# Feed-forward matmuls of a two-layer transformer block in other orders: two passes swapped, two tiles side by side

## The chip, the cores and the metric

The kernel runs on one core of a Trainium2 chip. Its engines are TensorE (PE, with its weight loads as PEld), VectorE (DVE), ScalarE (ACT), GpSimd (POOL) and SyncE (SP, which here only starts transfers). Each takes its own instructions in order and waits for the others by semaphores. The metric is the device time of one execution, in microseconds.

## What is computed

A sequence of 512 tokens with 1024 features passes through two layers, each with attention and a feed-forward part, and a last norm. The change touches the feed-forward part alone:

```python
def conv_ffn(h, w_in, conv_w, conv_b, w_out):      # w_in 1024 x 5632, w_out 2816 x 1024
    u = h @ w_in
    up = jnp.pad(u, ((0, 0), (CONV_WIDTH - 1, 0), (0, 0)))
    c = conv_b + conv_w[0] * up[:, 0:s]
    for i in range(1, CONV_WIDTH):
        c = c + conv_w[i] * up[:, i:i + s]
    a, gate_in = jnp.split(c, 2, axis=-1)
    return (jax.nn.silu(a) * gate_in) @ w_out

h = h + conv_ffn(rms_norm(h, norm_ffn[layer]), ...)
```

## The kernel before

All activations lie with features on the 128 partitions and the 512 tokens along the free axis. Every operand of the large products is split in two parts, high and low, of a narrower kind of float (fp32r), and `mm3` (line 101) computes a product in three matmuls, or passes, that add up in one bank of PSUM: high by high (line 102), high weight by low activation (line 103), low weight by high activation (line 104). The weight is the stationary operand, so each pass loads it anew.

`weight` (line 110) brings one tile of 128 x 1024 weights: a transfer into `wr` (three buffers, line 115), a cast on ACT into the high part `wh` (three buffers, line 116), and a subtraction for the low part `wl` (three buffers, line 117), in the feed-forward of layer 1 always on POOL. A cast can start when the transfer has landed and PE has read the last of what the buffer held before.

`ffn` (line 378) runs for each layer. Its hidden features are done in two halves. In each half 11 pairs of tiles (a feature tile and its gate tile, `fin`) are multiplied with the normed input `x`, one weight tile after the other, 8 contraction chunks by 3 passes, so 24 matmuls of 512 columns to a weight tile; the pair's results lie in the two banks of one `pss` tile, which has two buffers. DVE scales them (line 412), ACT and DVE apply the convolution (lines 414 to 417), ACT the silu (line 420), and the product is split again into `actv` (lines 198 and 199). Then come the output products of that half (`product`, line 427): for each of 8 output tiles 11 chunks by 3 passes into one `pst` bank (three buffers), which DVE adds to `h` (line 443). Their weights (`fout`) are 11 tiles of 8 blocks each, block number f * 11 + k, so a weight tile serves parts of two output tiles.

The program is written in this order, and a scheduler then places the instructions of each engine: it may move some ahead of others when it expects an operand to be late. The result is a fixed order for each engine.

Of the kernel before, what the change touches and what calls it, by code (L numbers as in the profile page):

```python
# [17 lines left out]
P = 128  # L18
S = 512
D = 1024  # L20
NCH = D // P
# [12 lines left out]
# which of Pool (P) and DVE (V) takes a subtraction or sum that either can: the low parts of the weights, in  # L34
# order (layer 0, layer 1), and of other operands
# [4 lines left out]
# where the steps of the attention phases go among one another, in units of quads (four heads of a token tile)  # L40
# [10 lines left out]
# where the norm of the first half of the tokens goes in the products of the second half  # L51
# [4 lines left out]
# columns of the constant table  # L56
# [5 lines left out]
# columns of the mask table  # L62
# [10 lines left out]
def hybrid_kernel(ctx, tc, t):  # L73
# [73 lines left out]
    def warm_exp(dep):  # L147
        # the exponential's table, loaded ahead of its first use
        act(small.tile([P, 1], F32, name="warm", bufs=1), dep, AF.Exp, scale=0.0)

# [12 lines left out]
    def token_scale(ssq=None):  # L163
        """1 / rms of each token, [P, NT] with tokens on partitions."""
# [10 lines left out]
    def spread_scale(r_nat):  # L175
        """The same along the free axis, on every partition, in PSUM."""
        ps = t_tile()
        for i in range(NT):
            mm(ps[:, i * P:(i + 1) * P], r_nat[:, i:i + 1].to_broadcast([P, P]), ident, start=True, stop=True)
        return ps  # L180
# [7 lines left out]
    def weave(*lists):  # L188
        """Emit lists of steps side by side, each in its own order; (steps, first, last) places one."""
# [28 lines left out]
    # in four steps, one token tile and one bank each  # L218
# [22 lines left out]
    # or in four steps along the contraction, two token tiles to a bank  # L241
# [24 lines left out]
    def split_v(dst, src, r):  # L266
        # dst [P, g, 2, 64] f32r, src [P, g, 64] in PSUM
# [4 lines left out]
    def cat_k(pool, k, n):  # L272
        # k [P, n, 64] natural -> the same as hi|lo
# [4 lines left out]
    def stack_k(dst, kc, n):  # L278
        # -> dst [(hi|lo, d), n, P]
# [26 lines left out]
    def probs_t(pool, blocks, way="V"):  # L306
        # four [P, P] blocks -> split [key, head, query]
# [15 lines left out]
    def heads_out(pool, ot, pv, quad, i):  # L323
        # pv [(hi|lo, d), 4 heads * P] -> ot [(head parity, d), chunk, hi/lo, token]
# [11 lines left out]
    def out_proj(h, ot, ws, half, last):  # L336
# [21 lines left out]
        def early():  # L358
            # the first half of the heads, for four feature tiles
# [18 lines left out]
    def ffn(layer, gi, h, slots, before, last, end=None):  # L378
        with tc.tile_pool(name=f"ffn{layer}", bufs=1) as fp:
# [9 lines left out]
            for half in range(2):  # L389
                acts = []  # L390
                for j in range(HPAIR):
                    jj = half * HPAIR + j
                    ps = s_tile()
                    for s in range(2):
                        hi, lo = weight(t["fin"][layer, 2 * jj + s])
                        hv = hi.rearrange("p (k n) -> p k n", k=NCH)
                        lv = lo.rearrange("p (k n) -> p k n", k=NCH)
                        for c in range(NCH):
                            mm3(ps[:, s], hv[:, c], lv[:, c], x[c][:, 0], x[c][:, 1],
                                c == 0, c == NCH - 1)  # L400
                    if jj == 0:
# [4 lines left out]
                    for s in range(2):  # L406
                        src = ps[:, s]
                        if jj == 0:
                            # the scale comes later than the first pair
# [17 lines left out]
                def product(ps, f, toks, ks):  # L427
                    for k in ks:
# [4 lines left out]
                        col = slice(b % 8 * P, (b % 8 + 1) * P)  # L433
                        mm3(ps, hi[:, col], lo[:, col], acts[k][:, 0, toks], acts[k][:, 1, toks],
                            k == 0, k == HPAIR - 1)

                for f in range(NCH):
                    if half == 1 and f == NCH - 1 and end:
# [8 lines left out]
    # ================= layer 0 attention =================  # L447
    x = x_pair(["s1", "s2"])

    with tc.tile_pool(name="att_a", bufs=1) as pa, tc.tile_pool(name="att_a2", bufs=1) as pp:  # L450
# [9 lines left out]
        # one key-value group: its four query heads, and its keys and values of both branches  # L460
# [105 lines left out]
        def compress(kv):  # L566
# [50 lines left out]
            def third():  # L617
# [3 lines left out]
                # [Vh | Vl] below the blocks of hi and of lo probabilities, zero for the other head  # L621
# [32 lines left out]
        def quad_a(g, i):  # L654
            nb = i + 1
            # the compressed keys in front of the others, where they fit in the same banks
# [111 lines left out]
            def ctrans():  # L768
                # rows (head parity, hi/lo, block)
# [46 lines left out]
        def ahead(n):  # L816
            # the softmax of quad n, the queries of quad n + 1, the copy of those of quad n + 2
# [27 lines left out]
    # ================= layer 0 feed forward =================  # L845
# [5 lines left out]
    def after_a(f):  # L851
        # the inputs of layer 1, feature tile by feature tile
# [11 lines left out]
    # ================= layer 1 attention =================  # L864
# [121 lines left out]
    # ================= layer 1 feed forward and the final norm =================  # L986
# [4 lines left out]
    def finale(product):  # L991
        # the last feature tile in two halves of the tokens, and the norm of each at once
# [15 lines left out]
        def sums(a):  # L1008
            # the squares of the other feature tiles
# [94 lines left out]
def _halves(w):  # L1104
    # [1024, 1024] -> (half, f pair) tiles of [P, 2 f, 4 k, P]
# [4 lines left out]
def _layout(a):  # L1110
# [21 lines left out]
    # (a_j, gate_j) feature tiles in turn  # L1132
# [26 lines left out]
```

## Time and profile before

| what | value |
|---|---|
| runs | 1299.46 and 1537.13 us, median 1418.3 us |
| the profiled execution, its span | 1298.1 us |
| PE busy | 1251.8 us (96%) |
| weight loads on PE | 1041.9 us (80%) |
| DVE busy | 831.9 us (64%) |
| ACT busy | 629.9 us (49%) |
| POOL busy | 661.4 us (51%) |

Times in the trace count from the span's start. Layer 0's feed-forward takes about 375 to 740, layer 1's about 898 to 1290. A row of the timeline is an instruction (or several alike in a row) with its start, its duration and, in brackets, how long its engine had been idle and what ended that. Matmuls overlap, so the time that one takes of PE is the step from its start to the next one's. PEclk is the granted clock as a share of 2.4 GHz; 0.50 is 1.2 GHz.

### The profile page before, as it was taken

To read this page: it belongs to the slowest core of one execution; us is meant where nothing else is said; L and a number is where in the kernel's file an instruction comes from. 1 tells how busy PE (TensorE), PEld (TensorE's weight loads), DVE (VectorE), ACT (ScalarE), POOL (GpSimd) and SP (SyncE) were. 2 spreads that over 40 slices of the span, in tenths; PEclk is the share of its full clock that TensorE was granted. 3 is DMA by queue.
4 is the path that set the end of the run, shared out by engine and by line. 5 is a ranking of instruction groups with operands and counts; after the bars stand their busy time and mean duration, and the time that the engine had idled before them with its cause. 6 is when DMAs were issued, how large, how long until landed. Compare 5 with 4: busy or idle time off the path is not lost.

```text
span 1298.1 us, 17657 instructions
## 1 busy us (share of the span) xinstructions
PE 1251.8 (96%) x6539; PEld 1041.9 (80%) x6539; DVE 831.9 (64%) x1331; ACT 629.9 (49%) x1278; POOL 661.4 (51%) x536
## 2 busy tenths in 40 slices
PE   8988999999999999999999999899999999999997
PEld 7887787878778888888888898777788888888886
DVE  5877868787458775047776458775497730577712
ACT  4555867777454443124444347665454421344332
POOL 6425767766484444444445446664644444444452
PEclk9998999999999999999999999999999999999999
DMA  5342011121122222222222131111222222232221
GB/s 187 115 155 80 1 34 34 34 98 34 33 97 91 88 97 98 97 88 91 98 98 97 49 115 33 34 65 49 98 82 98 98 97 95 84 97 98 97 82 65
DMA packets 34085, 106.45 MB, mean 82 GB/s; under 512 B 4048, under 2 KB 6608, under 8 KB 34000
## 3 DMA queue, kind: packets, MB, share of 16 engines
q1 hardware_dynamic: 34000, 105.34, 24.1%
q8 instruction: 51, 0.84, 0.3%
q14 instruction: 34, 0.28, 0.1%
HBM read 103.23 MB, written 2.10 MB: 81 GB/s over the span
## 4 chain that ended last, share of the span: by engine, by line
PE 86%; DVE 8%; ACT 3%; issue 1%; DMA 1%; SPq 0%; POOL 0%; DVEq 0%; ACTq 0%; POOLq 0%
PE pss L103 14%; PE pss L104 14%; PE pss L102 14%; PE pst L102 10%; PE pst L104 10%; PE pst L103 10%; PE pst L310 3%; DVE s L185 2%; PE psv L765 1%; PE pss L713 1%; PE psv L764 1%; PE pss L714 1%; PE pst L300 1%; DVE s L347 1%; DVE nmx L725 1%
## 5 line engine op out<-in xcount | busy, mean ns | idle before, releaser
L117 POOL TENSOR_TENSOR wl<-wr,wh 128x1024 fp32r<-128x1024 f32 (+1 forms) x173 | 406.3, 2350 | 437.8 <-ACT wh L116 434.5
L116 ACT CAST wh<-wr 128x1024 fp32r<-128x1024 f32 (+2 forms) x201 | 197.7, 985 | 347.6 <-issue 173.1
L103 PE MATMUL pss<-s,wh 128*128 128x512 f32 x736 | 292.0, 397 | 3.8 <-DVE s L185 3.8
L102 PE MATMUL pss<-s,wh 128*128 128x512 f32 x736 | 291.3, 396 | 2.3 <-ACT s L198 2.1
L104 PE MATMUL pss<-s,wl 128*128 128x512 f32 x736 | 290.8, 396 | 0.0
L103 PEld LDWEIGHTS pss<-s,wh 128*128 128x128 f32 x736 | 138.3, 188 | 39.5 <-DVE s L185 6.2
L102 PEld LDWEIGHTS pss<-s,wh 128*128 128x128 f32 x736 | 138.1, 188 | 37.1 <-ACT s L198 3.0
L104 PEld LDWEIGHTS pss<-s,wl 128*128 128x128 f32 x736 | 138.3, 188 | 32.6
L104 PE MATMUL pst<-actv,wl 128*128 128x512 f32 (+1 forms) x363 | 141.0, 389 | 0.0
L103 PE MATMUL pst<-actv,wh 128*128 128x512 f32 (+1 forms) x363 | 140.7, 388 | 0.0
L102 PE MATMUL pst<-actv,wh 128*128 128x512 f32 (+1 forms) x363 | 140.3, 386 | 0.0
L415 DVE SCALAR_TENSOR_TENSOR cv<-u,convp,cv 128x512 f32<-128x512 f32 x88 | 123.2, 1439 | 13.4 <-ACT cv L414 13.4
L199 DVE TENSOR_TENSOR actv<-sa,actv 128x512 fp32r<-128x512 f32 x44 | 101.6, 2312 | 30.7 <-ACT actv L198 30.5
L443 DVE TENSOR_TENSOR s<-s,pst 128x512 f32<-128x512 f32 x31 | 21.3, 687 | 155.4 <-PE pst L104 155.4
L412 DVE TENSOR_TENSOR u<-pss,R 128x512 f32<-128x512 f32 x84 | 54.1, 686 | 64.5 <-PE pss L104 64.5
L420 ACT ACTIVATE sa<-cv 128x512 f32<-128x512 f32 x44 | 27.9, 634 | 123.1 <-DVE cv L417 123.0
L103 PEld LDWEIGHTS pst<-actv,wh 128*128 128x128 f32 x363 | 68.4, 188 | 15.2
L102 PEld LDWEIGHTS pst<-actv,wh 128*128 128x128 f32 x363 | 68.4, 188 | 14.8
L104 PEld LDWEIGHTS pst<-actv,wl 128*128 128x128 f32 x363 | 68.4, 188 | 13.9
L314 ACT CAST pth<-pst 128x512 fp32r<-128x512 f32 x92 | 53.7, 594 | 35.0 <-PE pst L310 30.9
L315 DVE TENSOR_TENSOR ptl<-pst,pth 128x512 fp32r<-128x512 f32 x92 | 62.2, 683 | 12.8 <-ACT pth L314 11.9
L414 ACT ACTIVATE cv<-u,convp 128x512 f32<-128x512 f32 x88 | 66.6, 807 | 2.2 <-DVE u L412 2.2
(242 smaller groups left out, 2634.4 us busy)
## 6 DMA issues: line engine op xcount, KB each, us to landing
wr<-fin SPq DMA_DIRECT2D x88, 512.0 KB, 3.3
wr<-fout SPq DMA_DIRECT2D x44, 512.0 KB, 3.2
wr<-wg SPq DMA_DIRECT2D x10, 512.0 KB, 3.3
wr<-cw SPq DMA_DIRECT2D x8, 512.0 KB, 3.4
wr<-woA SPq DMA_DIRECT2D x8, 512.0 KB, 3.8
wr<-woB SPq DMA_DIRECT2D x8, 512.0 KB, 3.3
wr<-wqb SPq DMA_DIRECT2D x6, 512.0 KB, 3.3
s<-xT SPq DMA_DIRECT2D x8, 256.0 KB, 5.3
```

The source lines that it names most:

```text
L102: mm(out, ah, bh, start=start, stop=False)
L103: mm(out, ah, bl, start=False, stop=False)
L104: mm(out, al, bh, start=False, stop=stop)
L116: nc.scalar.copy(hi[:, :n], raw[:, :n])
L117: engines[next(pick["w"], "P")].tensor_sub(lo[:, :n], raw[:, :n], hi[:, :n].bitcast(F32))
L199: engines[pick["split"][name] if name else "V"].tensor_sub(lo, src, hi.bitcast(F32))
L310: pe_tr(ps[:, r * P:(r + 1) * P], blocks[r], ident)
L314: nc.scalar.copy(ph, ps)
L315: nc.vector.tensor_sub(pl, ps, ph.bitcast(F32))
L412: nc.vector.tensor_mul(u[:, s, 2:], src, norm["R"])
L414: act(cv[:, s], u[:, s, 2:], AF.Identity, bias=par[:, 3:4], scale=par[:, 2:3])
L415: nc.vector.scalar_tensor_tensor(cv[:, s], u[:, s, 1:S + 1], par[:, 1:2], cv[:, s], op0=OP.mult, op1=OP.add)
```

## The change

Three places in `ffn` get another order; the arithmetic stays.

In layer 1 the first products of a pair are written side by side: for each chunk the passes are high by high, low weight by high, high weight by low, each for both tiles of the pair before the next pass, so that the two banks are written in turn. In layer 1's first half the output products are written in the same way for two output tiles at a time. In layer 0's first half the output products keep their one bank, but the second and third pass change places.

```diff
+                    pair = []
                     for s in range(2):
-                        hi, lo = weight(t["fin"][layer, 2 * jj + s])
-                        hv = hi.rearrange("p (k n) -> p k n", k=NCH)
-                        lv = lo.rearrange("p (k n) -> p k n", k=NCH)
+                        pair.append([z.rearrange("p (k n) -> p k n", k=NCH)
+                                     for z in weight(t["fin"][layer, 2 * jj + s])])
+                        if layer == 1:
+                            continue
+                        hv, lv = pair[s]
                         for c in range(NCH):
                             mm3(ps[:, s], hv[:, c], lv[:, c], x[c][:, 0], x[c][:, 1],
                                 c == 0, c == NCH - 1)
+                    if layer == 1:
+                        for c in range(NCH):
+                            for w, xx in ((0, 0), (1, 0), (0, 1)):
+                                for s in range(2):
+                                    mm(ps[:, s], pair[s][w][:, c], x[c][:, xx], start=c == 0 and (w, xx) == (0, 0),
+                                       stop=c == NCH - 1 and xx == 1)
...
+                        if half == 0 and layer == 0:
+                            mm(ps, hi[:, col], acts[k][:, 0, toks], start=k == 0, stop=False)
+                            mm(ps, lo[:, col], acts[k][:, 0, toks], start=False, stop=False)
+                            mm(ps, hi[:, col], acts[k][:, 1, toks], start=False, stop=k == HPAIR - 1)
+                            continue
                         mm3(ps, hi[:, col], lo[:, col], acts[k][:, 0, toks], acts[k][:, 1, toks],
                             k == 0, k == HPAIR - 1)

                 for f in range(NCH):
+                    if half == 0 and layer == 1:
+                        if f % 2:
+                            continue
+                        pq = [t_tile(), t_tile()]
+                        for k in range(HPAIR):
+                            for w, xx in ((0, 0), (1, 0), (0, 1)):
+                                for z in range(2):
+                                    b = (f + z) * HPAIR + k
+                                    if b // 8 not in wts:
+                                        wts[b // 8] = weight(t["fout"][layer, half, b // 8])
+                                    mm(pq[z], wts[b // 8][w][:, b % 8 * P:(b % 8 + 1) * P], acts[k][:, xx],
+                                       start=k == 0 and (w, xx) == (0, 0), stop=k == HPAIR - 1 and xx == 1)
+                        for z in range(2):
+                            nc.vector.tensor_add(h[:, f + z], h[:, f + z], pq[z])
+                        continue
```

How the instructions stand on PE and ACT shows what the scheduler made of it. In the rows below a name's number tells buffers' uses apart: a `wh` and the `wl` with the next number are the two parts of one weight tile, and `pss` with one number is one pair. The semaphore of the engine that is waited for stands in brackets.

On PE, in the first half of layer 1, where a pair ends and the next begins. Before:

```order
L102 MATMUL pss_9978<-s3_9243,wh_10010 128x512
L103 MATMUL pss_9978<-s3_9243,wh_10010 128x512
L104 MATMUL pss_9978<-s3_9243,wl_10011 128x512
L102 MATMUL pss_10056<-s0_9242,wh_10058 128x512 [waits DVE_49,Activation_49]
L103 MATMUL pss_10056<-s0_9242,wh_10058 128x512
L104 MATMUL pss_10056<-s0_9242,wl_10059 128x512 [waits Pool_49]
L102 MATMUL pss_10056<-s0_9242,wh_10058 128x512
L103 MATMUL pss_10056<-s0_9242,wh_10058 128x512
L104 MATMUL pss_10056<-s0_9242,wl_10059 128x512
```

After the change, the same place of another pair:

```order
L409 MATMUL pss_9744<-s3_9243,wh_9746 128x512
L409 MATMUL pss_9744<-s3_9243,wh_9752 128x512
L409 MATMUL pss_9822<-s0_9242,wh_9830 128x512 [waits Activation_49]
L409 MATMUL pss_9822<-s0_9242,wl_9825 128x512 [waits Pool_49]
L409 MATMUL pss_9900<-s0_9242,wh_9902 128x512 [waits DVE_49,Activation_49]
L409 MATMUL pss_9822<-s0_9242,wl_9831 128x512 [waits Pool_49]
L409 MATMUL pss_9822<-s0_9242,wh_9824 128x512
L409 MATMUL pss_9822<-s0_9242,wh_9830 128x512
L409 MATMUL pss_9822<-s0_9242,wh_9824 128x512
L409 MATMUL pss_9822<-s0_9242,wh_9830 128x512
```

Before, the next tile waits once for each of its parts and then serves 24 matmuls alone. Now the last matmuls of a pair read both of its tiles (`wh_9746`, `wh_9752`), and behind them stand a matmul of the next pair's second tile (`wh_9830`), one of the first tile's low part (`wl_9825`), one of the pair after that (`pss_9900`, `wh_9902`), and one of the second tile's low part (`wl_9831`); each of the four waits.

On ACT, around the same place after the change (`cv`, `sa` and `actv` belong to the pairs that PE has ended):

```order
L116 CAST wh_9824<-wr_9823 128x1024 [waits DMAHW5_49,PE_49,Pool_49]
L424 ACTIVATE cv_9729<-u_9727,convp_81 128x512 [waits DVE_49] x2
L430 ACTIVATE sa_9738<-cv_9729 128x512 [waits DVE_49]
L198 CAST actv_9741<-sa_9738 128x512 [waits DVE_49]
L116 CAST wh_9830<-wr_9829 128x1024 [waits DMAHW6_49,PE_49,Pool_49]
L116 CAST wh_9902<-wr_9901 128x1024 [waits DMAHW7_49,PE_49,Pool_49]
L424 ACTIVATE cv_9807<-u_9805,convp_81 128x512 [waits DVE_49] x2
L430 ACTIVATE sa_9816<-cv_9807 128x512 [waits DVE_49]
L198 CAST actv_9819<-sa_9816 128x512 [waits DVE_49]
```

And before:

```order
L116 CAST wh_10010<-wr_10009 128x1024 [waits DMAHW2_49,PE_49,Pool_49]
L198 CAST actv_9897<-sa_9894 128x512 [waits DVE_49]
L116 CAST wh_10058<-wr_10057 128x1024 [waits DMAHW3_49,PE_49,Pool_49]
L414 ACTIVATE cv_9963<-u_9961,convp_81 128x512 [waits DVE_49] x2
L420 ACTIVATE sa_9972<-cv_9963 128x512 [waits DVE_49,Activation_49]
L116 CAST wh_10088<-wr_10087 128x1024 [waits DMAHW4_49,PE_49,Pool_49]
L198 CAST actv_9975<-sa_9972 128x512 [waits DVE_49]
L116 CAST wh_10136<-wr_10135 128x1024 [waits DMAHW5_49,PE_49,Pool_49]
```

Before, the casts alternate with the steps on a finished pair, one every half pair. Now two casts stand together, `wh_9830` and `wh_9902`, both with a wait for PE, ahead of the steps on the finished pair.

On PE, output products of layer 1's first half after the change, where the second bank (`pst_10291`) has its first matmul:

```order
L464 MATMUL pst_10290<-actv_9975,wh_10293 128x512
L464 MATMUL pst_10290<-actv_10053,wh_10293 128x512
L464 MATMUL pst_10290<-actv_10053,wl_10294 128x512
L464 MATMUL pst_10290<-actv_10053,wh_10293 128x512
L464 MATMUL pst_10291<-actv_9507,wh_10300 128x512 [waits Activation_49]
L464 MATMUL pst_10290<-actv_10131,wh_10300 128x512
L464 MATMUL pst_10378<-actv_9507,wh_10336 128x512 [waits Activation_49]
L464 MATMUL pst_10291<-actv_9507,wl_10301 128x512 [waits Pool_49]
L464 MATMUL pst_10291<-actv_9507,wh_10300 128x512
L464 MATMUL pst_10291<-actv_9585,wh_10300 128x512
L464 MATMUL pst_10291<-actv_9585,wl_10301 128x512
```

The 24 matmuls ahead of the second bank's first one (the first four rows here are their end) are all in the first bank (`pst_10290`) and on one weight tile (`wh_10293`, `wl_10294`); the scheduler has moved them ahead of the second bank's, which in the source stand between them.

## Rows read from the trace of the kernel before

**Rows 1.** The page: busy time of an engine, its granted clock, the chain that ended last.
```profile
PE 1251.8 (96%) x6539; PEld 1041.9 (80%) x6539; DVE 831.9 (64%) x1331; ACT 629.9 (49%) x1278; POOL 661.4 (51%) x536
...
PEclk9998999999999999999999999999999999999999
...
PE 86%; DVE 8%; ACT 3%; issue 1%; DMA 1%; SPq 0%; POOL 0%; DVEq 0%; ACTq 0%; POOLq 0%
PE pss L103 14%; PE pss L104 14%; PE pss L102 14%; PE pst L102 10%; PE pst L104 10%; PE pst L103 10%; PE pst L310 3%; DVE s L185 2%; PE psv L765 1%; PE pss L713 1%; PE psv L764 1%; PE pss L714 1%; PE pst L300 1%; DVE s L347 1%; DVE nmx L725 1%
```

**Rows 2.** Windows: from:to, length, busy us of PE, PEld, DVE, ACT, POOL; PEclk; DMA.
```profile
495.00:555.00 60.00, 60.00 (x259) 48.61 (x258) 13.47 (x16) 13.72 (x15) 26.41 (x11) 1.00 0.28 92
...
952.00:1040.00 88.00, 88.00 (x379) 70.84 (x378) 71.04 (x79) 38.05 (x51) 38.49 (x16) 1.00 0.28 94
...
sum 373.00, PE 373.00 PEld 301.77 DVE 203.94 ACT 130.38 POOL 170.53; mean PE 74.60 PEld 60.35 DVE 40.79 ACT 26.08 POOL 34.11
```

**Rows 3.** Timeline of PE in layer 1: start us, duration us, engine, line, operation.
```profile
999.84 0.40 PE L103 MATMUL pss<-s,wh 128*128 128x512 f32 x1
...
1011.97 0.40 PE L104 MATMUL pss<-s,wl 128*128 128x512 f32 x1
```

**Rows 4.** Who waited for whom in 952:1105, longest first: total us, times, longest us.
```profile
POOL wl L117 <- ACT wh L116: 89.1, 28, 4.8
DVE s L443 <- PE pst L104: 46.9, 8, 7.0
```

**Rows 5.** Timeline of all engines where a weight tile gives way to the next.
```profile
996.34 0.40 PE L103 MATMUL pss<-s,wh 128*128 128x512 f32 x1
...
996.81 1.05 ACT L116 CAST wh<-wr 128x1024 fp32r<-128x1024 f32 x1 [3.60 <-issue]
...
997.94 2.41 POOL L117 TENSOR_TENSOR wl<-wr,wh 128x1024 fp32r<-128x1024 f32 x1 [2.78 <-ACT wh L116]
```

**Rows 6.** Timeline where PE waits for the low part of a weight tile.
```profile
89.40 0.68 DVE L117 TENSOR_TENSOR wl<-wr,wh 128x512 fp32r<-128x512 f32 x1
...
90.14 0.19 PEld L103 LDWEIGHTS pss<-wl,s 128*128 128x128 f32 x1 [0.39 <-DVE wl L117]
90.14 0.39 PE L103 MATMUL pss<-wl,s 128*128 128x256 f32 x1 [0.25 <-DVE wl L117]
...
90.37 0.28 PE L104 MATMUL pss<-wh,s 128*128 128x256 f32 x1
...
90.48 0.28 PE L102 MATMUL pss<-wh,s 128*128 128x256 f32 x1
```

**Rows 7.** Timeline of PE in output products of layer 0, second half, passes mixed.
```profile
690.02 0.39 PE L103 MATMUL pst<-actv,wh 128*128 128x512 f32 x1
...
690.71 0.39 PE L103 MATMUL pst<-actv,wh 128*128 128x512 f32 x1
690.94 0.39 PE L102 MATMUL pst<-actv,wh 128*128 128x512 f32 x1
691.17 0.39 PE L104 MATMUL pst<-actv,wl 128*128 128x512 f32 x1
...
692.54 0.39 PE L102 MATMUL pst<-actv,wh 128*128 128x512 f32 x1
```

**Rows 8.** Windows around two falls of the granted clock and one stretch without.
```profile
262.80:266.20 3.40, 1.56 (x16) 1.39 (x14) 3.35 (x5) 3.15 (x9) 2.22 (x2) 1.00 1.02 410
266.20:269.60 3.40, 3.40 (x13) 2.69 (x14) 2.45 (x6) 1.81 (x6) 2.33 (x4) 0.50 0.52 212
...
781.60:785.00 3.40, 1.86 (x16) 1.54 (x14) 2.68 (x6) 2.07 (x9) 3.11 (x6) 1.00 0.79 240
...
819.10:822.60 3.50, 0.61 (x3) 0.48 (x4) 3.47 (x5) 1.37 (x7) 2.01 (x2) 0.99 0.34 89
822.60:826.00 3.40, 3.40 (x17) 3.30 (x16) 1.69 (x6) 1.82 (x7) 2.23 (x5) 0.50 0.16 65
826.00:829.40 3.40, 3.40 (x29) 3.27 (x29) 1.46 (x5) 0.88 (x2) 0.90 (x2) 1.00 0.00 0
```

## The prediction

> **What bounds the kernel now.** I read the page's busy times first. TensorE (PE) is busy 96% of the span, and the slices of its granted clock stand at 9 tenths or more nearly throughout, so nearly all of the time runs at the upper of its two levels, 2.4 GHz [rows 1]. The page's chain of work that ended last gives PE 86% of the span, most of it lines 102 to 104, which are the three passes of `mm3` [rows 1]. Then I cut out the feed-forward stretches by windows: in the five of them PE is busy in every microsecond, 373 of 373, while DVE, ACT and POOL leave gaps [rows 2]. So in the stretches that the change touches there is nothing but PE: any idle time put there is added to the end, and any change of the matmuls' pace counts in full.
>
> The pace I took from the timeline of PE in layer 1: 53 matmuls start from 999.84 to 1011.97, that is 52 steps of 0.2333 us; one lasts 0.40 us, so they overlap [rows 3]. The list of who waited for whom in that stretch has no wait of PE at all; its longest is POOL's subtraction waiting for ACT's cast of the weights, 89.1 us in 28 waits [rows 4]. That is spare time on POOL: weights are made ready well ahead of their use. Why that is so is the heart of the matter. A weight tile passes through ACT (cast to the high part, line 116) and POOL (low part, line 117) and there are three buffers of each part. Before, PE uses one tile for 24 matmuls (5.6 us) and goes on to the next. When it lets go of a buffer, two finished tiles are still ahead of it, 11.2 us of work, and the new one is ready after a cast and a subtraction, about 1.05 and 2.41 us [rows 5]. The cover is some 7.6 us.
>
> **The change, part by part.** No matmul, load or cast is added or removed; only orders change.
>
> *First products of layer 1 (22 pairs of tiles, 48 matmuls each, 1056 in all).* A pair's two tiles are now used in turn to the last matmul. Both buffers come free together at the end of the pair, and one spare is left for the next pair, which needs two tiles at once. Its second tile can be cast only when the pair has ended. The order on ACT shows this: two casts stand one behind the other, each with a wait for PE, and behind them wait this pair's two convolution steps. On PE the order shows what can be done meanwhile: after the last two matmuls of the pair come four that each wait for a cast or for POOL, and the last of them (the low part of the second tile) holds everything behind it.
>
> I count from the start of the last matmul but one, the last reader of the first buffer's high part. It ends after 0.40 [rows 3]. ACT starts 0.07 later: a matmul started at 996.34, so it ended at 996.74, and the cast that waited for that tile began at 996.81 [rows 5]. The cast takes 1.05. POOL starts 0.08 after it (997.86 to 997.94) and takes 2.41 [rows 5]. From the end of such a subtraction to PE's weight load it takes 0.06 (it started at 89.40, lasted 0.68, and the load began at 90.14), and the matmul behind that load is followed 0.23 later by the next instead of 0.11, so 0.12 is lost there [rows 6]. Sum: 0.40 + 0.07 + 1.05 + 0.08 + 2.41 + 0.06 + 0.12 = 4.19 us. Without a wait that matmul, the fifth after the one counted from, would start after 5 x 0.2333 = 1.17 us. The stall is **3.0 us**, once for each pair but the first, whose tiles are made ready during the layer's out projection: 21 x 3.0 = **63 us**.
>
> Nothing hides it, since PE is the chain. ACT's casts come ahead of the convolution steps (line 414), so a pair's output appears about 2 us later on ACT; DVE then has a whole pair, now 14 us, for its work, and it was busy 71 of 88 us before [rows 2]; PE's own wait for DVE's evacuation falls inside the stall. In the first pair the norm's scale (a square root on ACT, a reciprocal on DVE, a spread on PE) now stands between the waiting casts; I add 1 us for it, from nothing to the size of one cast.
>
> *Output products of layer 1, first half (264 matmuls).* By the source four pairs of output tiles would meet the same trouble, since a pair spans three weight tiles. But the scheduler has pulled the order apart: on PE the first 24 matmuls all go to the first bank, on one weight tile, and only then does the second bank's first one wait for a cast. 24 matmuls are 5.6 us against 3.5 for cast and subtraction, so the wait is covered; I take 0. If the cover failed, four joints of 3.0 us would cost 12.
>
> *Passes swapped in layer 0, first half (264 matmuls).* The low part is wanted one matmul (0.23 us) earlier; the cover there is the 7.6 us above, so 0. A gain or loss of pace would have to come from the order itself. The trace has a place where the scheduler had already mixed the passes (690.02 to 692.54, twelve matmuls with lines 102, 103, 104 out of turn): the eleven steps are 0.229 on average and none stands out [rows 7]. If the swap brought the pace from 0.2333 to 0.229, 264 x 0.0043 = 1 us would be gained. I take 0.
>
> *Pace in two banks.* In layer 1 each matmul now goes to another bank than the one before, and two in turn share their moving operand. The trace has no long stretch like that at full pace. Bounds: the fastest pace seen is the 0.229 just named [rows 7], which over 1320 matmuls is worth 6 us; 512 columns at 2.4 GHz take 0.213, which would be worth 26 us. I take 0.2333, since that is what the very same shapes do now, and since mixed passes changed nothing.
>
> The Trainium skill, page "TensorE: Matmul & The Clock Gate", section "Back-to-back issue gap", gives N/2.4 + 2.5 ns between matmuls, 216 ns for 512 columns. The row here says 233, so by the page there would be something to win; if the new order won it, 1320 x 0.0175 = 23 us would come off the sum.
>
> *The clock.* It is granted by halves, and PE's idle time can cost it. It fell to 0.50 after 262.80:266.20 (PE busy 1.56 of 3.40) and after 819.10:822.60 (0.61 of 3.50), and not after 781.60:785.00 (1.86 of 3.40) [rows 8]. A stretch at 0.50 then holds 17 matmuls where the next at 1.00 holds 29: 3.4 x (1 - 17/29) = 1.4 us lost; an exact half would be 1.7; I take 1.5. The new stalls leave PE three single matmuls in about 3.8 us, near the two stretches after which it fell, but broken up, and the stretch before and after is full. So the bounds are no fall and 21 falls (32 us). I take five, a quarter of the stalls: **8 us**.
>
> The Trainium skill, same page, section "A second HAM failure mode: psum-queue depth-cycling", tells of a kernel in which cycling through banks left PE short idles and the clock went up and down. By that rule the falls would come at most of the stalls.
>
> **Sum.** 63 + 1 + 0 + 0 + 8 = 72 us. The profiled execution has a span of 1298.1 us; the lower of the two runs is 1299.46, which fits it with 1.4 us around the span. The other run is 1537.13, so the median, 1418.3, lies between two different things, and nothing in the profile speaks of the second. I forecast what compares with 1299.5: 1299.5 + 72 = **1372 us**, 5.5% longer.
>
> **Rivals.**
> *The clock falls at most stalls.* For it: the two stretches above. Against it: three matmuls break each stall. With 21 falls: 1299.5 + 64 + 32 = 1395 us.
> *The stall is there, and the two banks bring a faster pace.* At 0.216, 23 us come back: 1372 - 23 = 1349. Against it: [rows 7] shows a pace that doesn't mind the order.
> *The waits are covered after all (the other side).* The cast of the second tile would have to be done before the pair has ended, as it would if a third buffer were free at that time. For it: POOL and ACT have spare time [rows 4]. Against it: in the order both casts wait for PE. The sum would be 1299.5 plus at most a gain of pace: 1276 at 0.216, 1299 at the present one. It is not slower from the point where the gain of pace pays the stall: 64 us over 1320 matmuls are 0.048 us each, a pace of 0.185, which is below the 0.213 that 512 columns need at 2.4 GHz. So only covered waits can do it, not the pace.
>
> **How the numbers follow.** Forecast with up to some ten falls of the clock: 0.78 (1358 to 1380: the low end with no fall and the pace of 0.229). Clock falls at most stalls: 0.12 (1380 to 1395). Faster pace with the stall: 0.05 (1341 to 1357). Covered waits: 0.05 (1276 to 1299). The range from 1356 to 1396 holds the first two, with 0.1 left out. About 2% is what a measurement of this kernel can tell from no change; 2% above 1299.5 is 1325. The covered case is within 2% (0.04), or faster if all of the pace comes too (0.01); all else is slower: 0.95.
>
> **What would show it.** In the profile after: PE idle of about 3 us before the first low-part pass of each pair in layer 1, put down to POOL's line 117 and ACT's line 116, 21 times, and the same 48 matmuls between; layer 1's first products longer by a quarter, all else in place; layer 0's swapped half as long as before; output products of layer 1's first half without idle time; single slices with PEclk below 9 in layer 1. I would be wrong if PE stayed 96% busy, if the steps between matmuls in layer 1 went well below 0.23, or if the clock stood at half through much of layer 1.

## The result: 1366.5 us, and where the 67 us lie

The changed kernel takes 1366.5 us (median of 1365.63 and 1367.41), against 1299.46 for the kernel before: a ratio of 1.052 (95% interval 1.048 to 1.057). The other run of before, 1537.13, is one of the slow ones that the kernel has now and then, so neither it nor the median of 1418.3 is used. The profiled execution has a span of 1365.6 us; before it was 1298.1. So +67.5 us stand against the +72 of the forecast.

The page of the profile after: busy time of the engines, the granted clock by slices, and the chain that ended last, by engine and by line.

```profile
PE 1275.1 (93%) x6539; PEld 1045.1 (77%) x6539; DVE 823.2 (60%) x1331; ACT 632.0 (46%) x1278; POOL 669.4 (49%) x536
...
PEclk9998999999999999999999999998999999999999
...
PE 69%; issue 12%; DVE 7%; POOL 6%; ACT 5%; DMA 1%; SPq 0%; DVEq 0%; ACTq 0%; POOLq 0%
PE pss L409 9%; PE pss L103 7%; PE pss L102 7%; PE pss L104 7%; PE pst L102 7%; PE pst L104 6%; PE pst L103 6%; POOL wl L117 6%; PE pst L310 3%; DVE s L185 2%; PE pst L445 2%; PE pst L447 2%; PE pst L446 2%; ACT wh L116 1%; PE psv L796 1%
```

Against [rows 1], PE's share of the chain has gone from 86% to 69%. What is new on the chain, or has grown, is POOL's line 117 (6%), ACT's line 116 and "issue" (12% after 1%). The count of matmuls is the same. PE's busy time has grown by 23 us all the same: a matmul with nothing right behind it counts with its whole 0.40 us, one behind a wait with 0.50, and one at 1.2 GHz longer still.

Windows after: from:to, length, then busy us of PE, PEld, DVE, ACT, POOL, the granted clock, DMA share and GB/s.

```profile
495.00:555.00 60.00, 60.00 (x259) 48.57 (x258) 13.57 (x16) 14.01 (x15) 25.69 (x11) 1.00 0.29 97
898.00:1050.00 152.00, 131.69 (x512) 98.78 (x510) 83.12 (x95) 57.92 (x77) 63.24 (x29) 0.94 0.21 70
987.80:991.20 3.40, 1.65 (x5) 0.86 (x6) 2.13 (x4) 2.85 (x4) 2.84 (x2) 1.00 0.02 5
991.20:994.60 3.40, 3.40 (x10) 2.63 (x9) 3.40 (x3) 0.00 (x0) 2.31 (x1) 0.50 0.51 164
1130.00:1285.00 155.00, 131.68 (x516) 97.07 (x515) 77.49 (x87) 47.45 (x60) 55.59 (x23) 0.98 0.22 72
```

Layer 0's swapped half (495:555) is full as in [rows 2], with the same 259 matmuls in 60 us. Layer 1's first products are not: 20 us of 152 idle, 23 us of 155. The third and fourth rows are a stall and a stretch at 1.2 GHz behind it.

The timeline after, at the end of one pair of weight tiles in layer 1 (start us, duration, engine, line, operation, in brackets the idle time ahead and what ended it):

```profile
958.45 0.63 PE L409 MATMUL pss<-s,wh 128*128 128x512 f32 x2
958.92 2.00 ACT L116 CAST wh<-wr 128x1024 fp32r<-128x1024 f32 x2 [4.61 <-PE pss L409]
...
960.02 0.50 PE L409 MATMUL pss<-s,wh 128*128 128x512 f32 x1 [0.94 <-ACT wh L116]
960.04 5.19 POOL L117 TENSOR_TENSOR wl<-wr,wh 128x1024 fp32r<-128x1024 f32 x2 [8.99 <-ACT wh L116]
...
960.98 0.50 PE L409 MATMUL pss<-s,wh 128*128 128x512 f32 x1 [0.22 <-ACT wh L116]
...
962.47 0.19 PEld L409 LDWEIGHTS pss<-s,wl 128*128 128x128 f32 x1 [1.31 <-POOL wl L117]
962.47 0.50 PE L409 MATMUL pss<-s,wl 128*128 128x512 f32 x1 [0.99 <-POOL wl L117]
```

This is the chain that the prediction drew: matmuls end, two casts start at 958.92 on the buffers just freed, POOL subtracts from 960.04, PE goes on at 962.47. From the second of the matmuls in the first row, which starts at 958.68, to the one at 962.81 behind the last, the steps are 1.34, 0.34, 0.61, 1.50 and 0.34 us where five of 0.2333 would do. The excess is 2.96 us, once per pair: the next pairs show the same steps at 972.84, 986.99 and so on, twenty times in all (three of them are shorter, 2.7 to 2.9 us). (The bracket shows less than the stall, since the profile lets a matmul last 0.40 us while its successor would start after 0.23.)

The list of waits of PE in 898:1290 after, the first four of eight (who waits for whom: total us, times, longest):

```profile
PE pss L409 <- ACT wh L116: 22.5, 38, 1.0
PE pss L409 <- POOL wl L117: 19.8, 20, 1.0
PE pss L102 <- ACT s L198: 2.1, 1, 2.1
PE pst L168 <- POOL acc L161: 2.0, 1, 2.0
```

In [rows 4] PE had no such wait; there it was POOL that waited for work.

### The profile page after: what moved, and what is told of

It reads as the page before. It is cut to its first block, busy times and chain, and to the rows that moved or that the text cites. A ratio compares the mean times of both kernels' runs of the same rounds, so it can differ in the third digit from the quotient of the medians.

```text
span 1365.6 us, 17638 instructions
## 1 busy us (share of the span) xinstructions
PE 1275.1 (93%) x6539; PEld 1045.1 (77%) x6539; DVE 823.2 (60%) x1331; ACT 632.0 (46%) x1278; POOL 669.4 (49%) x536
## 4 chain that ended last, share of the span: by engine, by line
PE 69%; issue 12%; DVE 7%; POOL 6%; ACT 5%; DMA 1%; SPq 0%; DVEq 0%; ACTq 0%; POOLq 0%
PE pss L409 9%; PE pss L103 7%; PE pss L102 7%; PE pss L104 7%; PE pst L102 7%; PE pst L104 6%; PE pst L103 6%; POOL wl L117 6%; PE pst L310 3%; DVE s L185 2%; PE pst L445 2%; PE pst L447 2%; PE pst L446 2%; ACT wh L116 1%; PE psv L796 1%
## 5 line engine op out<-in xcount | busy, mean ns | idle before, releaser
L117 POOL TENSOR_TENSOR wl<-wr,wh 128x1024 fp32r<-128x1024 f32 (+1 forms) x173 | 413.7, 2400 | 502.1 <-ACT wh L116 498.8
L409 PE MATMUL pss<-s,wh 128*128 128x512 f32 x704 | 209.9, 411 | 22.5 <-ACT wh L116 22.5
L409 PEld LDWEIGHTS pss<-s,wh 128*128 128x128 f32 x704 | 136.5, 194 | 69.8 <-ACT wh L116 39.1
L425 DVE SCALAR_TENSOR_TENSOR cv<-u,convp,cv 128x512 f32<-128x512 f32 x88 | 149.3, 1734 | 33.9 <-ACT cv L424 33.9
L102 PE MATMUL pss<-s,wh 128*128 128x512 f32 x384 | 152.7, 399 | 2.2 <-ACT s L198 2.1
L103 PE MATMUL pss<-s,wh 128*128 128x512 f32 x384 | 153.0, 398 | 1.9 <-DVE s L185 1.9
L104 PE MATMUL pss<-s,wl 128*128 128x512 f32 x384 | 152.3, 397 | 0.0
L409 PE MATMUL pss<-s,wl 128*128 128x512 f32 x352 | 118.7, 409 | 19.8 <-POOL wl L117 19.8
L103 PEld LDWEIGHTS pss<-s,wh 128*128 128x128 f32 x384 | 72.6, 189 | 20.4 <-DVE s L185 3.1
L102 PEld LDWEIGHTS pss<-s,wh 128*128 128x128 f32 x384 | 72.3, 189 | 20.7 <-ACT s L198 3.0
L199 DVE TENSOR_TENSOR actv<-sa,actv 128x512 fp32r<-128x512 f32 x44 | 67.8, 1543 | 30.5 <-ACT actv L198 30.5
L474 DVE TENSOR_TENSOR s<-s,pst 128x512 f32<-128x512 f32 x23 | 15.8, 688 | 105.6 <-PE pst L104 58.7
L103 PE MATMUL pst<-actv,wh 128*128 128x512 f32 (+1 forms) x187 | 70.9, 379 | 0.0
L102 PE MATMUL pst<-actv,wh 128*128 128x512 f32 (+1 forms) x187 | 70.6, 378 | 0.2 <-ACT wh L116 0.2
L104 PE MATMUL pst<-actv,wl 128*128 128x512 f32 (+1 forms) x187 | 70.4, 378 | 0.0
```

What stands on the lines that cost most here:

```text
L102: mm(out, ah, bh, start=start, stop=False)
L103: mm(out, ah, bl, start=False, stop=False)
L104: mm(out, al, bh, start=False, stop=stop)
L117: engines[next(pick["w"], "P")].tensor_sub(lo[:, :n], raw[:, :n], hi[:, :n].bitcast(F32))
L199: engines[pick["split"][name] if name else "V"].tensor_sub(lo, src, hi.bitcast(F32))
L409: mm(ps[:, s], pair[s][w][:, c], x[c][:, xx], start=c == 0 and (w, xx) == (0, 0), stop=c == NCH - 1 and xx == 1)
```

## Experiments

**The fourth buffer.** The parts of the weights rotate through four buffers in layer 1's feed-forward; `fp` is that layer's own pool.

```diff
-        hi = wsp.tile([P, WT], F32R, name="wh")
-        lo = wsp.tile([P, WT], F32R, name="wl")
+        pick["n"] = pick.get("n", 0) + 1
+        extra = pick.get("extra") if pick["n"] % 4 == 0 else None
+        hi = (extra or wsp).tile([P, WT], F32R, name="wh4" if extra else "wh")
+        lo = (extra or wsp).tile([P, WT], F32R, name="wl4" if extra else "wl")
...
+            if layer == 1:
+                pick["extra"] = fp
```

> The changed kernel with one edit: in layer 1's feed forward the hi and low parts of the weights rotate through four buffers instead of three (the fourth pair lies in the feed forward's own pool; two spare buffers of actv are given up for it). Theory (the second tile of a pair waits for the first tile's buffer, which is read to the end of the pair): with four buffers both tiles of the next pair are there before the pair ends, the 21 stalls of 2.96 us go, and the falls of the granted clock that stood at five of them go with them: 1366 - 62 - 8 = 1296, between 1292 and 1304; the waits of PE for wh and wl in the pairs of layer 1 are gone and the step stays at 0.2333. Rival one (the order itself is slower, by the two banks or by the changed sequence of weights, buffers or not): stays within 10 of 1366. Rival two (the stalls go, but the clock falls for another reason): 1304, with the granted clock of layer 1's pairs still below 0.97.

Measured: 1296.86 us, 0.998 of before (0.997 to 0.999). The waits of PE in 895:1285 of that run, all there are:

```profile
PE pss L102 <- ACT s L200: 2.1, 1, 2.1
PE psv L1054 <- ACT sq L1039: 1.0, 1, 1.0
PE pst L102 <- DVE s L349: 0.2, 1, 0.2
```

No wait for `wh` or `wl` is left, the granted clock is 1.00 in the windows of layer 1's first products, and the steps there are 0.2333. The kernel before also gains something from four buffers (the last of the experiments below); against that run, from the end of layer 1's attention to its second half's first products, this one takes 203.7 us after 204.3. So the order in two banks costs nothing by itself and gains no pace; the loss was the buffer, and the clock fell with the stalls.

**Which part of the change.** Two runs, each with part of the change as in the kernel before: one keeps only the first products of layer 1 side by side, the other keeps only the swapped passes and the paired output products.

```diff
 # only the first products side by side
-                        if half == 0 and layer == 0:
+                        if False:
...
-                    if half == 0 and layer == 1:
+                    if False:
 # without them
-                        if layer == 1:
-                            continue
...
-                    if layer == 1:
-                        for c in range(NCH):
...
```

> Of the three parts of the change only the first products of layer 1 side by side; the swapped passes of layer 0 and the paired output products of layer 1 are as before. Theory: the whole loss is here, 1366, and 1.4 more if the shorter step of the output products in the changed kernel (0.2289 instead of 0.2333, 264 of them) belongs to their own order: 1364 to 1370. Rival (the paired output products add to the loss through their two weight tiles): some 5 to 12 us less, 1354 to 1361.

> The other two parts of the change alone: swapped passes in one output half of layer 0, paired output products in one output half of layer 1; the first products of layer 1 as before. Theory: neither part costs anything. 1298 to 1300, with the output products of layer 1's first half at 0.2289 a step (-1.2 us) and those of layer 0's at 0.2333. Rival (a part of the loss belongs to the output products): 1304 to 1312, with waits of PE for wh or wl in them.

Measured: 1364.74 us (1.051 of before, 1.050 to 1.053) and 1299.13 us (1.0007, 0.9997 to 1.0016). The whole loss belongs to the first products. In the second of these runs PE is busy in 61.00 of 61.00 us in the swapped half of layer 0 (495:556) and in the paired half of layer 1 (1043:1104). The one thing that the theory expected and did not come is the shorter step of the paired products: they ran at 0.2333 in this run (below).

**How long before it is needed.** The first tile of a pair runs ahead of the second by one input tile, then by two (the 1 in the diff becomes a 2), with three buffers. That both frees its buffer earlier and puts off the need for the second tile.

```diff
-                        for c in range(NCH):
+                        for step in range(NCH + 1):
                             for w, xx in ((0, 0), (1, 0), (0, 1)):
                                 for s in range(2):
+                                    c = step - 1 * s
+                                    if not 0 <= c < NCH:
+                                        continue
```

> The changed kernel, three buffers, but in layer 1's pairs the first tile runs one input tile (three matmuls) ahead of the second: it is read out three matmuls before the pair's end, and the next pair begins with three matmuls that need no new tile. Theory: the last low part is needed 11 steps after the last read of the buffer it goes into, instead of 5, so each of the 21 stalls falls from 2.96 by 6 x 0.2333 = 1.40 to 1.6 us: 1366 - 29 = 1337, down to 1328 if the falls of the granted clock go too. Rival one (the stall is not the low part's but a fixed cost of each pair in this order): 1366. Rival two (the stall is decided by the cast's place in ScalarE's queue, not by the buffer): between 1355 and 1366.

> The same with a lead of two input tiles. Theory: 17 steps of 0.2333 = 3.97 us lie between the last read and the need, against 4.19 that the refill takes: 0.2 us a pair are left, 1366 - 21 x 2.74 - 8 (the falls of the clock) = 1300, between 1297 and 1309, without a byte more memory. Rival one: 1366. Rival two: between 1340 and 1366.

Measured: 1331.3 us (1.025 of before, 1.024 to 1.027) and 1304.0 us (1.005, 1.003 to 1.007). The timeline of PE at the same place in the run with a lead of one:

```profile
971.31 0.40 PE L412 MATMUL pss<-s,wl 128*128 128x512 f32 x1
972.01 0.47 PE L412 MATMUL pss<-s,wh 128*128 128x512 f32 x1 [0.31 <-DVE u L425]
973.24 0.50 PE L412 MATMUL pss<-s,wl 128*128 128x512 f32 x1 [0.76 <-POOL wl L117]
973.58 0.39 PE L412 MATMUL pss<-s,wh 128*128 128x512 f32 x1
```

Steps of 0.70, 1.23 and 0.34 give 1.57 over three normal ones, as expected (1.6). Part of the stall has changed its name: the first of the two is now put down to DVE, which has to take the finished pair out of the bank that a hoisted matmul wants (0.3 us, 17 times). With a lead of two, what is left at a boundary are two steps of about 0.34, some 0.2 us; only where the second half begins is there a longer one, of 1.46. The timeline of PE in that run at a boundary, where the second and the third row show the two steps:

```profile
976.03 0.40 PE L412 MATMUL pss<-s,wl 128*128 128x512 f32 x1
976.26 0.40 PE L412 MATMUL pss<-s,wh 128*128 128x512 f32 x1
976.61 0.50 PE L412 MATMUL pss<-s,wl 128*128 128x512 f32 x1
976.95 0.86 PE L412 MATMUL pss<-s,wh 128*128 128x512 f32 x3
```

No fall of the clock stands behind the shorter stalls in the profiled execution of either run: the windows of layer 1's second half with a lead of one have 1.00, and the one fall in its first half (0.50 from 931.5 to 934.9) is at the first pair, by the norm's products. So the time follows the distance between release and need, chunk by chunk, and no more memory is needed for most of the cure.

**A longer refill.** POOL makes the low part twice.

```diff
         engines[next(pick["w"], "P")].tensor_sub(lo[:, :n], raw[:, :n], hi[:, :n].bitcast(F32))
+        if twice:
+            nc.gpsimd.tensor_sub(lo[:, :n], raw[:, :n], hi[:, :n].bitcast(F32))
```

> The changed kernel, with the subtraction that makes the low part of each weight tile of layer 1's first products done twice on GpSimd, one after the other, the second with the same result. Theory: the subtraction lies on the path from the buffer's release to the waiting matmul, so each of the 21 stalls grows by one subtraction, 2.4 us: 1366 + 50 = 1416, between 1410 and 1426. Rival (the path ends with ScalarE's cast, or the order is slow by itself): GpSimd has room for it (49% busy), 1366 to 1372.

Measured: 1520.8 us, 1.172 of before (1.170 to 1.174). The direction is the theory's, and the rival, 1366 to 1372, is out. But the size is three times what I expected. The timeline of that run at a boundary shows why:

```profile
1001.59 5.12 POOL L117 TENSOR_TENSOR wl<-wr,wh 128x1024 fp32r<-128x1024 f32 x2 [10.96 <-ACT wh L116]
...
1006.67 5.57 POOL L119 TENSOR_TENSOR wl<-wr,wh 128x1024 fp32r<-128x1024 f32 x2
...
1009.51 0.80 PE L411 MATMUL pss<-s,wl 128*128 128x512 f32 x1 [6.49 <-POOL wl L119]
1009.67 0.76 PEld L411 LDWEIGHTS pss<-s,wh 128*128 128x128 f32 x2
...
1010.10 0.63 PE L411 MATMUL pss<-s,wh 128*128 128x512 f32 x1
```

POOL works first at both tiles' first subtraction (line 117, two in 5.12 us) and then at the second ones (line 119). The tile that PE waits for gets its second subtraction third, not second, so its path is longer by two subtractions and more: the step into that matmul is 6.99 us, against 1.50. That is 5.5 us instead of 2.4. Seventeen boundaries have that step and three a smaller one (6.1, 4.3 and 3.9 us); all the long steps at these twenty boundaries, clock aside, add up to 111 us more than in the changed kernel. The clock does much of the rest. Windows of layer 1's first products in this run:

```profile
912.00:1145.00 233.00, 152.53 (x529) 113.72 (x528) 125.78 (x100) 55.64 (x73) 120.54 (x49) 0.79 0.15 52
1211.00:1441.00 230.00, 149.03 (x507) 110.03 (x506) 121.58 (x91) 48.64 (x62) 112.98 (x43) 0.79 0.15 51
```

The mean clock is 0.79, and steps of 0.427 us, the lower level's, stand behind every stall: 22 stretches of 5 to 13 matmuls, which cost 38 us by the steps' excess over 0.2333, against 7.6 in the changed kernel. 111 and 30 are 141 of the 154 us by which this run is longer than the changed kernel; the other 12 are at layer 1's first pair, with two steps of 5.9 and 5.2 us.

**The first pair.** The fourth buffer's run was faster than the kernel before, by 1.8 us in the runs and 3.3 us in the traces between the last matmul of layer 1's attention and its first output product (142.1 after 145.4). The timeline of PE in the kernel before, at layer 1's first pair, has what went:

```profile
916.31 0.50 PE L103 MATMUL pss<-s,wh 128*128 128x512 f32 x1 [0.21 <-DVE s L185]
...
917.57 0.50 PE L103 MATMUL pss<-s,wh 128*128 128x512 f32 x1 [0.30 <-DVE s L185]
...
920.25 0.50 PE L102 MATMUL pss<-s,wh 128*128 128x512 f32 x1
922.13 0.50 PE L103 MATMUL pss<-s,wh 128*128 128x512 f32 x1 [1.38 <-DVE s L185]
```

PE waits there for input tiles that ACT and DVE still scale and split (line 185); the seven long steps are 3.05 us over seven normal ones. Layer 0's first pair has the same seven (368.77 to 375.57). Side by side, each input tile feeds six matmuls before the next is wanted, not three. Three kernels took that apart, all from the kernel before: only the first pair of each layer side by side, with four buffers; the same with three; and four buffers with no change of order.

```diff
-                        for c in range(NCH):
+                        if jj == 0:
+                            continue
+                        for c in range(NCH):
...
                     if jj == 0:
+                        for c in range(NCH):
+                            for w, xx in ((0, 0), (1, 0), (0, 1)):
+                                for s in range(2):
+                                    mm(ps[:, s], pair[s][w][:, c], x[c][:, xx],
+                                       start=c == 0 and (w, xx) == (0, 0), stop=c == NCH - 1 and xx == 1)
```

> The kernel before, with only the first pair of first products of each layer side by side, and four buffers in both feed forwards (two spare buffers of actv given up). In the kernel before TensorE waits in each layer's first pair for input tiles that are still being scaled and split (seven steps over length, 3.05 us in layer 1 and about 3.0 in layer 0); side by side each input tile feeds twice as many matmuls before the next is wanted, and in the run with the fourth buffer those steps were gone in layer 1. Theory: both go, 1298.6 - 6 = 1292.6, between 1290.5 and 1295. Rival one (what the fourth buffer's run gained over the kernel before comes from the buffer or from the paired output products): 1297 to 1299. Rival two (the sums of squares, which follow the first pair, become late instead): 1295 to 1298.

> The run with the first pair of each layer side by side again, but with the three buffers of the kernel before. Behind the first pair stand the products that sum the squares, on which TensorE waits anyway, so the refill of the buffer may be covered there. Theory: part of the one stall in each layer stays, as in the changed kernel, where the boundary behind layer 1's first pair cost about 1.5 us instead of 3.0: 1291.1 + 2 x 1.5 = 1294, between 1291 and 1297. Rival one (the sums cover it wholly): 1291. Rival two (they cover nothing, and the falls of the clock come with it): 1297 to 1301, no gain over the kernel before.

> The kernel before with four buffers of hi and low parts in both feed forwards (two spare buffers of actv given up) and no change of order. Theory (the gain of the run with the first pair side by side belongs to the order): 1298, as the kernel before, within 1.5, with the seven long steps in each layer's first pair where they were. Rival (it belongs to the fourth buffer): 1291 to 1294.

| kernel | us | ratio to before (95%) | attention to first output product, layer 0, layer 1 (us) |
|---|---|---|---|
| before | 1298.2 to 1298.8 | | 145.2, 145.4 |
| first pair, four buffers | 1291.1 | 0.995 (0.993 to 0.997) | 142.0, 142.1 |
| first pair, three buffers | 1294.3 | 0.996 (0.994 to 0.997) | 142.4, 142.6 |
| four buffers, old order | 1292.9 | 0.995 (0.994 to 0.997) | 143.8, 143.9 |

The last column is worked out from starts in the timelines. Waits of PE in 905:935 for the scaled inputs, in the kernel before and in the run with four buffers and the old order:

```profile
PE pss L103 <- DVE s L185: 1.9, 3, 1.4
```
```profile
PE pss L103 <- DVE s L187: 1.3, 3, 0.7
```

In the two runs with the first pair side by side there is none of these; the one wait in that window is for DVE, which adds up an earlier result of the out projection (line 349), with four buffers and with three:

```profile
PE pst L102 <- DVE s L349: 0.2, 1, 0.2
```
```profile
PE pst L102 <- DVE s L349: 0.7, 1, 0.7
```

The first pair side by side beats the kernel before by 0.4 to 0.5%, and needs no memory for it: with three buffers a layer takes 0.4 to 0.5 us more than with four, not the 1.5 that I expected. Nor does this lie at the boundary behind the pair, where no step is over 0.32 us in either run. It is the wait just shown, ahead of the pair: with four buffers two more of the pair's matmuls have been moved in front of it. So the boundary costs nothing, which was rival one's case. The reason is plain in hindsight: the pair that follows is used one tile after the other again, so its second tile is wanted 24 matmuls later. That the median met the forecast of 1294 is luck; the runs lie between 1289.5 and 1296.3, the profiled one at 1291.5. My theory that the gain belongs to the order alone fell, though. Four buffers with the old order gain as much in the runs: 1.4 to 1.5 us a layer in the first pair, where the long steps are now 2.2 us over instead of 3.05 and seven of the pair's matmuls already stand among the out projection's products (902.53 to 906.26), where a step of 0.91 us stood before, and 1.2 us a layer from a step of 0.2289 in the first half's output products, which nothing in the edit explains (below). For the first of these two the trace shows where it arises, for the second it shows no reason, and the intervals of the three kernels don't tell them apart.

## What held in the prediction, and the step that failed

**The step that failed** is the first pair of layer 1. The sum charged it with a refill stall of 3.0 us and 1 us for the norm, and put at nothing the waits that the pair already had; measured, it cost 4.4 us at the norm and gave back 3.05 of old waits, 1.35 in all instead of 4. The main mechanism, the refill stall of the other pairs, held.

**What bounds the kernel** held. Every idle microsecond put into PE came out at the end; no engine took over.

**The stall** was the right one at the right place: 2.96 us against the 4.19 - 1.17 = 3.0 of the sum, twenty times, 58.8 us with the three shorter ones. The lead of one and of two input tiles and the longer refill move both ends of that difference, the release and the need, and the time follows. What failed in the longer refill was my expectation of that run: I counted one more subtraction and had not read POOL's order.

**The first pair** was wrong in two ways. The boundary behind it has no refill stall: the twenty waits for `wl` in the list above are those of the other boundaries. PE waits there for the norm:

```profile
927.77 1.05 PE L168 MATMUL pst<-ones,acc 128*128 128x2 f32 x8 [1.96 <-POOL acc L161]
...
930.50 2.07 PE L179 MATMUL pst<-cst,r_nat 128*128 128x128 f32 x8 [0.88 <-DVE r_nat L172]
```

The first wait is for POOL's sum of the squares, which ends at 927.72. In the kernel before that sum ended no earlier, at 929.56, but there 25 matmuls of the next pair stand ahead of the norm's first products, and PE came to those at 933.66 without a wait; now a single one stands there. The second wait is for the reciprocal, and from 930.5 to 932.8 the granted clock is 0.50, so that the eight products of line 179 take 1.73 us instead of 0.80.

What the boundary cost as a whole follows from the starts. From the pair's first matmul behind the out projection to the end of the norm's products, the kernel before took 26.2 us (914.06 to 940.25) with 94 matmuls of first products done, the changed one 17.8 us (914.45 to 932.23) with 52. The 42 still to do are 9.8 us, so the changed kernel is 1.4 us behind there. As 3.05 us of the old waits for the inputs are gone, the boundary with the norm cost about 4.4. I had overlooked those old waits, which the sum has at nothing: they stand in the trace of before, but my windows of layer 1 began at 952, behind them. A change of order can repair a wait that it was not meant for.

**The falls of the clock.** Five pieces at 1.2 GHz stand behind stalls in layer 1's first products (from 932.8, 991.5, 1035.6, 1196.0 and 1240.5), of 7 to 9 matmuls, 1.35 to 1.73 us over the normal steps, 7.6 us in all. Five at 1.5, 8 us, was the forecast; the number five was a choice between 0 and 21, and its being met is luck as much as reading: the run with only the first products side by side, whose pairs have the same order, has seven. Ahead of the one in the windows above, PE was busy 1.65 of 3.40 us; of the twenty stalls sixteen had no fall behind them. With stalls of half the length there was none, with the longer refill one behind each. The rival with falls at most stalls is out for this kernel. The Trainium skill, page "TensorE: Matmul & The Clock Gate", section "A second HAM failure mode: psum-queue depth-cycling", tells of a clock that goes up and down as PE idles shortly between groups of matmuls. The run with the longer refill agrees (0.79), the changed kernel only in part (0.94 and 0.98).

**Pace.** Two banks in turn and a shared moving operand changed nothing in the first products: 0.2333 before, after, and with four buffers. The rival of 1349 is out, and so is a gain by the same page of the Trainium skill, section "Back-to-back issue gap": its 216 ns for 512 columns is reached nowhere here. (The section gives that figure for an isolated matmul and 131 ns for a stream of them, which is farther still.) The steps here are 229 and 233 ns on average, and no single one behind a 512-column matmul of the weights is under 224.

**Output products and swapped passes** cost nothing, as taken. The output products of layer 1's first half took 60.2 instead of 61.6 us from start to start, 1.4 less (1.2 by their step, the rest because one of them stands ahead), which I had at 0.

**The sum** by what was measured: 58.8 + 4.4 - 3.05 + 7.6 - 1.4 = 66.4, and 1.1 elsewhere, +67.5 us; forecast 63 + 1 + 8 = 72. Of the 4.5 us between them the first pair is the largest part (2.65, since 1.35 stand against 4), then the output products (1.4); the other stalls (1.2) and the falls (0.4) came out a little smaller, and the 1.1 elsewhere go the other way. The covered case, the rival on the other side, needed a buffer free before the pair ends. That is what the fourth buffer supplies, and 1296.86 lies in its range of 1276 to 1299.

## What to carry to other kernels

Before two streams of work are interleaved, count the buffers that both hold until the end: with N buffers, what matters is how many steps lie between the last read of a buffer and the first need of what goes into it next, against the refill's time. If it is short by a few steps, stagger the two streams by that much; it costs no memory. And interleave where the operand that both share arrives late, as in the first pair here, not everywhere.

## What the runs showed of the hardware

The same output products run at two steps, and keep one for the whole of a half: 0.2333 us, or 0.2289 (in turn about 0.225, 0.229 and 0.232). The order does not decide it. The paired order ran at 0.2289 in the changed kernel and with a lead of one, and at 0.2333 in the run with the fourth buffer; the old order at 0.2333 in the first halves of the kernel before, and at 0.2289 in its second halves, in the run with only the first products side by side and, in both layers, with four buffers and the old order. Timelines of PE in the changed kernel, and in the run with the fourth buffer, at the same products:

```profile
1075.96 0.39 PE L464 MATMUL pst<-actv,wl 128*128 128x512 f32 x1
1076.19 0.62 PE L464 MATMUL pst<-actv,wh 128*128 128x512 f32 x2
1076.65 0.39 PE L464 MATMUL pst<-actv,wl 128*128 128x512 f32 x1
```
```profile
1040.14 1.10 PE L468 MATMUL pst<-actv,wh 128*128 128x512 f32 x4
1041.07 0.63 PE L468 MATMUL pst<-actv,wl 128*128 128x512 f32 x2
1041.54 1.10 PE L468 MATMUL pst<-actv,wh 128*128 128x512 f32 x4
```

Three matmuls in 0.69 us there, six in 1.40 here (1040.14 to 1041.54), on the same shapes at the same clock. It is worth 1.2 us for 264 matmuls, and what sets it stays open; the first products kept 0.2333 in every run.
